# Indirect transfers pinned with their register moves, and the first four heads' queries loaded as float32 pairs, in a threshold-attention kernel

## The chip, the cores and the metric

The kernel runs on one core of one Trainium2 chip. The metric is the time of one execution on the device, in microseconds (us); less is better. Three timed runs of the kernel before gave 235.24, 236.1 and 237.11 us, median 236.1.

## The reference

```python
scores = np.einsum('bhqd,bhkd->bhqk', Q, K) * scale          # 8 batches, 12 heads, 512 x 512, dim 64
weights = np.exp(scores - np.max(scores, axis=-1, keepdims=True))
weights = weights / (np.sum(weights, axis=-1, keepdims=True) + 1e-10)
weights = np.where(weights > threshold, weights, 0)          # threshold 0.1
weights = weights / (np.sum(weights, axis=-1, keepdims=True) + 1e-10)
return np.einsum('bhqk,bhkd->bhqd', weights, V)
```

A softmax weight over 0.1 is rare among 512 keys, so nearly all rows of the output are zero.

## The kernel before

The kernel writes zeros over the whole output, finds the few rows that may hold a weight over the threshold, and works out those alone.

The 96 heads are handled in 48 pairs (`hp`) and 24 quads of heads (`hq`). For a pair, K arrives as float32 by two DMAs on the queue of SP (`load_k`, L209), is transposed on PE by matmuls with an identity (`do_ktr`, L333), copied from PSUM to SBUF as float32 (`kt`, by ACT at L317 or DVE at L319) and cast from there to float16 (`kf`, on POOL at L321). For a quad, Q arrives as float16 by one casting DMA on POOL's queue (`load_q`, L221), is brought into the layout of pairs (`qm`, POOL or DVE), transposed on PE (L370) and copied out (`qt`). Then, four times per pair, PE makes a 128 x 1024 tile of scores in PSUM (`sc`, L386), and ACT (L394, true exponential) or DVE (L396, an exponential by bits) makes the tile `e`; there are 192 such tiles. PE sums them against a small matrix (`groups`, L405), and DVE reduces the sums to one number per row (`stat`, L413).

For every eight heads (`j`, 12 of these groups) a chain of short steps follows, late behind the main stream: flags of the rows that pass, their rank, a list of row numbers (`idx`), then three indirect transfers, all on POOL's queue. The gather (L471) fetches the chosen rows of Q, their scores and exponentials are made anew (`xqk` L500, `xe` L507), the key is found (`junk` L518, `vidx` L525), the fetch (L536) brings the row of V into `vsel`, and the scatter (L542) writes it over the zeros of the output. A scatter waits for its `vsel` and for the two zero writes of its rows.

All steps are entered in a planner written in the kernel (`Schedule`): each has a list of engines with a cost in us, its predecessors, a due time, and the buffers that it takes and gives. The planner places the steps by greedy list scheduling; a list of random draws (`DRAWS`) shifts due times a little, and `LAG` sets how much later than the main stream the chains of the groups are due. The kernel then issues all steps in the order of the planned starts, and `keep` asks the recording layer to leave each engine's instructions in that order. An engine takes its instructions strictly in order, so one that waits holds up all behind it.

An indirect transfer comes with moves that set registers of POOL; only the transfer itself is given to `keep`. In the built program of before, the scatters do not stand where the planner put them: the plan has scatter `j` behind fetch `j+1` and two `kf` casts, while in the built order each scatter stands one to four instructions behind its own fetch. Gather and fetch have changed places in some groups.

At the start, K0 and K1 (the pairs of the first quad) are each loaded half by SP's and half by ACT's queue, and the first quad's Q by two casting DMAs on POOL. PE transposes K0 and K1 into one PSUM tile; DVE makes the two halves of `kt`, ACT casts both to `kf`; POOL and DVE make `qm`, PE transposes it, DVE makes `qt`. Then the first score tiles follow. Seven matmuls on zeros (`warm`, L263) run on PE before all of it.

Of the kernel before, what the change touches and what calls it, by code (L numbers as in the profile page):

```python
# [115 lines left out]
def kernel(  # L116
# [19 lines left out]
    nc = tc.nc  # L136
    B, H, S, D = Q.shape
    P = 128
    assert D == 64 and H % 4 == 0 and S == 4 * P and (B * H) % 8 == 0
    R = S // P  # L140
# [8 lines left out]
    f32 = mybir.dt.float32  # L149
    bf16 = mybir.dt.bfloat16  # L150
    f16 = mybir.dt.float16
# [35 lines left out]
    LAG, WARM = 8.0, 7  # L187
    DRAWS = (55125, 12429, 78892, 43664, 17346, 65358, 95610, 46971, 68712, 54930, 91140, 80100)
# [16 lines left out]
    T = {}  # L205

    def load_pair(dst, src, hp, other=nc.sync):
        for h, eng in ((0, nc.sync), (1, other)):
            eng.dma_start(out=dst[:, :, h, :], in_=src[hp][:, h])  # L209
# [6 lines left out]
    def load_q(hq, parts=1):  # L216
        q_sb = qload.tile([P, 4, R, D], f16)
        T["q", hq] = q_sb
        for i in range(parts):
            part = slice(i * 4 // parts, (i + 1) * 4 // parts)  # L220
            keep(nc.gpsimd.dma_start(out=q_sb[:, part].rearrange("p h r d -> p h (r d)"), in_=Q4[hq][:, part]))  # L221

    load_k(0, nc.scalar)
    load_q(0, 2)
    load_k(1, nc.scalar)
# [110 lines left out]
    def do_kev(hq, part, eng):  # L336
        if part != 1:
            kt = ktpool.tile([P, 2, S], f32)
            T["kt", hq] = kt
        n = slice(0, 2) if part is None else slice(part, part + 1)  # L340
        copy(eng, T["kt", hq][:, n], T["ktr", hq][:, n])
# [22 lines left out]
    def do_qtr(hq, part, eng):  # L364
        if part != 1:
            qp = mpsum.tile([P, 2, S], f16, name="smh", tag="sm")
            T["qtr", hq] = qp
        for n in range(2) if part is None else (part,):
            for r in range(R):
                keep(nc.tensor.matmul(T["qtr", hq][:, n, r * P:(r + 1) * P],  # L370
                                      lhsT=T["qm", hq][:, n, r].rearrange("p h d -> p (h d)"),
                                      rhs=identity_h[:], is_transpose=True, start=True, stop=True))

    def do_qev(hq, part, eng):
        if part != 1:
            qt = qtpool.tile([P, 2, S], f16)
            T["qt", hq] = qt
        n = slice(0, 2) if part is None else slice(part, part + 1)
        copy(eng, T["qt", hq][:, n], T["qtr", hq][:, n])
# [90 lines left out]
    def do_gather(j, eng):  # L470
        keep(nc.gpsimd.indirect_dma_start(  # L471
            out=qsel_bufs[j % NS][:], out_offset=None, in_=Qr,
            in_offset=bass.IndirectOffsetOnAxis(ap=T["idx", j][:, 0:1], axis=0),
            element_offset=j * 8 * S * D, bounds_check=8 * S - 1, oob_is_err=False))
# [60 lines left out]
    def do_fetch(j, eng):  # L535
        keep(nc.gpsimd.indirect_dma_start(  # L536
            out=T["vsel", j][:], out_offset=None, in_=Vr,
            in_offset=bass.IndirectOffsetOnAxis(ap=T.pop(("vidx", j))[:, 0:1], axis=0),
            element_offset=j * 8 * S * D, bounds_check=8 * S - 1, oob_is_err=False))

    def do_scatter(j, eng):
        i = nc.gpsimd.indirect_dma_start(  # L542
            out=Or, out_offset=bass.IndirectOffsetOnAxis(ap=T.pop(("idx", j))[:, 0:1], axis=0),
            in_=T.pop(("vsel", j))[:], in_offset=None, element_offset=j * 8 * S * D,
            bounds_check=8 * S - 1, oob_is_err=False)
        keep(i)
        T["scat", j] = i
# [24 lines left out]
    add("numbers", {"POOL": (1.5, 1.6)}, [("q", 0)], -3.0, do_numbers)  # L572
    add("casts", {"DVE": (1.3, 1.5)}, ["numbers"], 1.0, do_casts)
    for hq in range(NQ):
# [4 lines left out]
        for n, hp in enumerate(pairs):  # L579
            if hp < 2:  # L580
                add(("k", hp), {"SP": (0.7, 3.3)}, [], -30 + n, nothing)
            else:
                buf = [("ktr", hp - 6)] if hp >= 6 else [("ktr", max(0, hp // 2 - 1))]
                add(("k", hp), {"SP": (1.3, 4.0)}, buf, u0 - 26 + n, lambda e, hp=hp: load_k(hp))
        if hq == 0:
            add(("q", 0), {"POOL": (2.0, 4.5)}, [], -30, nothing)
        else:
            buf = [("qmix", 2 * hq - 5)] if hq >= 3 else [("qmix", 0)]
            add(("q", hq), {"POOL": (0.85, 5.5)}, buf, u0 - 20, lambda e, hq=hq: load_q(hq))
        add(("z", hq), {"SP": (2.0, 5.0)}, [("exp", 2 * hq, 0)], u0 + 4, lambda e, hq=hq: do_zero(hq, e))  # L590
        for n, hp in enumerate(pairs):
            add(("ktr", hp), {"PE": (0.44, 0.70)}, [("k", hp)] + (ahead if n == 0 else [("ktr", hp - 1)]), u0 - 9 + n * 0.1,
                lambda e, hp=hp: do_ktr(hp, e), takes=[("sc", ("ktr", hq))] if n == 0 else [])
            add(("qmix", hp), {"POOL": (0.57, 0.75), "DVE": (0.25, 0.40)}, [("q", hq)] + (ahead if n == 0 else [("qmix", hp - 1)]), u0 - 10,
                lambda e, hp=hp: do_qmix(hp, e), takes=[("qm", hq)] if n == 0 else [])
        if hq == 0:
            for n in range(2):
                add(("kev", 0, n), HALF, [("ktr", n)] + ([("kev", 0, 0)] if n else []), -8 + n, lambda e, n=n: do_kev(0, n, e),
                    takes=[] if n else [("kt", 0)], gives=[("sc", ("ktr", 0))])
                add(("qtr", 0, n), {"PE": (0.23, 0.44)}, [("qmix", n)] + ([("qtr", 0, 0)] if n else []), -8 + n,  # L600
                    lambda e, n=n: do_qtr(0, n, e), takes=[] if n else [("sm", ("qtr", 0))], gives=[("qm", 0)])
                add(("qev", 0, n), {"DVE": (0.35, 0.5), "ACT": (0.50, 0.72)}, [("qtr", 0, n)] + ([("qev", 0, 0)] if n else []), -7 + n,
                    lambda e, n=n: do_qev(0, n, e), takes=[] if n else [("qt", 0)], gives=[("sm", ("qtr", 0))])
        else:
            add(("kev", hq), UNIT, [("ktr", hp) for hp in pairs], u0 - 8, lambda e, hq=hq: do_kev(hq, None, e),
                takes=[("kt", hq)], gives=[("sc", ("ktr", hq))])
            add(("qtr", hq), {"PE": (0.45, 0.66)}, [("qmix", hp) for hp in pairs], u0 - 8, lambda e, hq=hq: do_qtr(hq, None, e),
                takes=[("sm", ("qtr", hq))], gives=[("qm", hq)])
            add(("qev", hq), {"DVE": (0.62, 0.80), "ACT": (0.93, 1.13)}, [("qtr", hq)], u0 - 7, lambda e, hq=hq: do_qev(hq, None, e),
                takes=[("qt", hq)], gives=[("sm", ("qtr", hq))])  # L610
        for n, hp in enumerate(pairs):
            kev, qev = (("kev", 0, n), ("qev", 0, n)) if hq == 0 else (("kev", hq), ("qev", hq))
            kf_engs = {"POOL": (0.60, 0.78)}
            if hq == 0:
                kf_engs = {"POOL": (0.60, 0.78), "DVE": (0.5, 0.7), "ACT": (0.5, 0.7)}
            add(("kf", hp), kf_engs, [kev] + ([("kf", hp - 1)] if n else []), u0 - 6 + 4 * n, lambda e, hp=hp: do_kf(hp, e),
                takes=[("kf", hq)] if n == 0 else [])
            for c in range(R):
                u = u0 + 4 * n + c
                add(("qk", hp, c), {"PE": (0.23, 0.45)}, [("kf", hp), qev], u - 3,  # L620
                    lambda e, hp=hp, c=c: do_qk(hp, c, e), takes=[("sc", ("qk", hp, c))],
                    gives=[("kf", hq), ("qt", hq)])
                add(("exp", hp, c), UNIT, [("qk", hp, c)], u,
                    lambda e, hp=hp, c=c: do_exp(hp, c, e), takes=[("e", (hp, c))], gives=[("sc", ("qk", hp, c))])
            for jj in range(C2):
                deps = [("exp", hp, c) for c in range(R)] if jj == 0 else [("d", hp, jj - 1)]
                add(("d", hp, jj), {"PE": (0.116, 0.31 if jj == C2 - 1 else 0.116)}, deps, u0 + 4 * n + 3 + 0.01 * jj,
                    lambda e, hp=hp, jj=jj: do_d(hp, jj, e), takes=[("sm", ("d", hp))] if jj == 0 else [],
                    gives=[("e", (hp, c)) for c in range(R)] if jj == C2 - 1 else [])
            add(("dred", hp), {"DVE": (0.61, 0.78)}, [("d", hp, C2 - 1)], u0 + 4 * n + 3.5,  # L630
                lambda e, hp=hp: do_dred(hp, e), gives=[("sm", ("d", hp))])
        qevs = [("qev", 0, 0), ("qev", 0, 1)] if hq == 0 else [("qev", hq)]
        add(("qsq", hq), SQUARE, qevs, u0 + 4, lambda e, hq=hq: do_square("q", hq, e), takes=[("qsq", hq)], gives=[("qt", hq)])
        add(("ksq", hq), SQUARE, [("kf", hp) for hp in pairs], u0 + 4, lambda e, hq=hq: do_square("k", hq, e),
# [144 lines left out]
```

## Time and profile before

| what | value |
|---|---|
| median of three runs | 236.1 us |
| the profiled execution's own time | 233.86 us |
| its span, first instruction to last | 232.0 us |
| mean granted clock of PE | 0.915 |
| busy: PE, DVE, ACT, POOL | 195.5, 186.8, 157.3, 125.7 us |
| weight loads of PE (PEld) | 126.3 us |
| first tile `e` starts, last one ends | 10.61, 209.06 us |
| indirect transfers, mean of one on POOL: gather, fetch, scatter | 1112, 1112, 1032 ns |

The profile is of one execution. Its span is 1.86 us less than that execution's own time, which in turn is 2.24 us under the median of the timed runs. Busy times are of the engines; the DMA engines run beside them. A line of the timeline gives the start in us, the duration, engine, line of the code, operation, tile written and tile read, and in brackets how long the engine had been idle just before and what ended that. In the chain of waits, each piece is the work, or the transfer, that the next one had to wait for; "issue" is time for which the profile shows no releaser. A q behind an engine's name is its queue, where instructions are issued and wait.

### The profile page before, as it was taken

The numbers are of one execution on the slowest core, as the hardware profiler recorded it, in microseconds if no ns is written. First come the engines' busy times: TensorE is split into PE (matmuls) and PEld (weight loads), VectorE is DVE, ScalarE is ACT, GpSimd is POOL, SyncE is SP. The second block draws the span as 40 slices with busy tenths as digits, with TensorE's granted clock in tenths as the row PEclk, the third lists the DMA queues.
The fourth block names the chain that finished last, engine by engine and source line by source line (L and its number), as shares of the span: only waits on it lengthen the run. The fifth ranks groups of instructions, "written<-read, shape, count | busy, mean of one in ns | idle before, by whom it ended". The sixth has DMA issues, their size and how long they took to land.

```text
span 232.0 us, 7237 instructions
## 1 busy us (share of the span) xinstructions
PE 195.5 (84%) x2997; PEld 126.3 (54%) x2997; DVE 186.8 (81%) x327; ACT 157.3 (68%) x186; POOL 125.7 (54%) x204
## 2 busy tenths in 40 slices
PE   6498998999669988998999799899889999798130
PEld 2255665666347655674666466566566657455000
DVE  5568999989566898899689798799889997998420
ACT  2378779787646786779659579698868787880010
POOL 4617335664473738573764663875584736413541
PEclk9779999999956999999799999999999999998555
DMA  6999999999989996547257186455563000000000
GB/s 129 202 233 360 198 202 359 322 263 335 328 258 285 288 214 109 86 105 129 33 113 141 43 120 124 99 78 110 81 125 79 11 0 7 9 5 4 9 2 13
DMA packets 68019, 32.54 MB, mean 140 GB/s; under 512 B 52278, under 2 KB 64706, under 8 KB 67984
## 3 DMA queue, kind: packets, MB, share of 16 engines
q1 hardware_dynamic: 53088, 24.91, 39.7%
q0 software_dynamic: 13840, 6.88, 22.8%
q8 instruction: 24, 0.39, 0.7%
q10 hardware_dynamic: 1056, 0.26, 0.5%
q14 instruction: 11, 0.09, 0.1%
HBM read 25.95 MB, written 12.98 MB: 168 GB/s over the span
## 4 chain that ended last, share of the span: by engine, by line
PE 48%; DVE 17%; DMA 11%; issue 8%; ACT 8%; POOL 6%; POOLq 0%; ACTq 0%; DVEq 0%
PE sm L405 15%; PE sc L386 14%; PE sc L333 8%; DMA vsel<-in_V_dram,vidx 8%; DVE e L396 7%; ACT e L394 5%; PE smh L370 3%; PE sm L429 3%; PE sm L500 3%; DVE stat L413 2%; DMA k_sb<-in_K_dram 2%; POOL out_dram L542 2%; DVE kt L319 2%; DVE ksq L353 2%; DMA qsel<-in_Q_dram,idx 1%
## 5 line engine op out<-in xcount | busy, mean ns | idle before, releaser
L394 ACT ACTIVATE e<-sc 128x1024 bf16<-128x1024 f32 x125 | 122.7, 1026 | 30.2 <-PE sc L386 27.3
L396 DVE TENSOR_SCALAR e<-sc 128x1024 int16<-128x1024 f32 x67 | 81.2, 1218 | 2.9 <-PE sc L386 1.7
L386 PE MATMUL sc<-qt,kf 64*128 64x512 f16 x384 | 67.4, 399 | 8.2 <-DVE e L396 3.6
L405 PEld LDWEIGHTS <-e 128*128 128x128 bf16 x1536 | 53.9, 100 | 25.5 <-issue 20.7
L405 PE MATMUL sm<-groups,e 128*128 128x64 bf16 x1536 | 63.3, 196 | 4.5 <-ACT e L394 1.8
L321 POOL CAST kf<-kt 128x512 f16<-128x512 f32 x46 | 29.2, 648 | 40.1 <-ACT kt L317 23.5
L413 DVE TENSOR_REDUCE stat<-sm 128x8 f32<-128x512 f32 x48 | 32.9, 686 | 13.8 <-PE sc L386 6.5
L333 PE MATMUL sc<-identity_f,k_sb 128*128 128x128 f32 x192 | 31.8, 296 | 1.4 <-DMA k_sb<-in_K_dram 1.4
L386 PEld LDWEIGHTS <-kf 64*128 64x128 f16 x384 | 17.0, 94 | 26.8 <-issue 18.2
L333 PEld LDWEIGHTS sc<-identity_f,k_sb 128*128 128x128 f32 x192 | 22.0, 149 | 7.2 <-issue 3.8
L221 POOL DMA_DIRECT2D q_sb<-in_Q_dram x25 | 20.7, 827 | 5.8 <-POOL qm L321 2.7
L321 POOL COPY qm<-q_sb 128x512 f16<-128x512 f16 x36 | 22.8, 653 | 1.8 <-DMA q_sb<-in_Q_dram 1.6
L542 POOL DMA_INDIRECT out_dram<-vsel,idx x12 | 12.4, 1032 | 20.7 <-DMA vsel<-in_V_dram,vidx 18.7
L370 PE MATMUL smh<-identity_h,qm 128*128 128x128 f16 x192 | 15.5, 221 | 4.6 <-DVE qt L319 2.0
L471 POOL DMA_INDIRECT qsel<-in_Q_dram,idx x12 | 13.3, 1112 | 9.4 <-DVE qb L479 3.6
L317 ACT COPY kt<-sc 128x1024 f32<-128x1024 f32 x13 | 13.2, 1014 | 6.0 <-PE sc L333 4.8
L536 POOL DMA_INDIRECT vsel<-in_V_dram,vidx x12 | 13.3, 1112 | 6.8 <-POOL vidx L525 2.6
L507 ACT ACTIVATE xe<-sm 128x512 f32<-128x512 f32 x12 | 7.2, 603 | 14.3 <-PE sm L500 14.3
L317 ACT COPY qt<-smh 128x1024 f16<-128x1024 f16 x12 | 12.2, 1013 | 6.8 <-PE smh L370 4.5
L319 DVE COPY kt<-sc 128x1024 f32<-128x1024 f32 (+1 forms) x12 | 13.5, 1132 | 3.9 <-PE sc L333 3.9
L353 DVE TENSOR_SCALAR ksq<-kf 128x1024 int16<-128x1024 int16 x24 | 13.8, 576 | 3.4 <-POOL kf L321 3.4
L370 PEld LDWEIGHTS <-qm 128*128 128x128 f16 x192 | 11.4, 98 | 8.4 <-DVE qm L319 3.4
(85 smaller groups left out, 176.8 us busy)
## 6 DMA issues: line engine op xcount, KB each, us to landing
out_dram<-zero SPq DMA_DIRECT2D x24, 512.0 KB, 7.0
k_sb<-in_K_dram SPq DMA_DIRECT2D x94, 128.0 KB, 4.8
q_sb<-in_Q_dram POOLq DMA_DIRECT2D x23, 256.0 KB
k_sb<-in_K_dram ACTq DMA_DIRECT2D x2, 128.0 KB
q_sb<-in_Q_dram POOLq DMA_DIRECT2D x2, 128.0 KB
qsel<-in_Q_dram,idx POOLq DMA_INDIRECT x12
vsel<-in_V_dram,vidx POOLq DMA_INDIRECT x12
out_dram<-vsel,idx POOLq DMA_INDIRECT x12
```

Of the source, the lines that this page charges most:

```text
L221: keep(nc.gpsimd.dma_start(out=q_sb[:, part].rearrange("p h r d -> p h (r d)"), in_=Q4[hq][:, part]))
L317: keep(nc.scalar.copy(dst, src))
L319: keep(nc.vector.tensor_copy(dst, src))
L321: keep(nc.gpsimd.tensor_copy(dst, src))
L333: keep(nc.tensor.matmul(T["ktr", hq][:, n, r * P:(r + 1) * P], lhsT=k_sb[:, r, :, :].rearrange("p h d -> p (h d)"), rhs=identity_f32[:], i ...
L353: keep(nc.vector.tensor_scalar(sq[:].bitcast(i16), src[:].bitcast(i16), 0x7FFF, 2, op0=ALU.bitwise_and, op1=ALU.logical_shift_right))
L370: keep(nc.tensor.matmul(T["qtr", hq][:, n, r * P:(r + 1) * P], lhsT=T["qm", hq][:, n, r].rearrange("p h d -> p (h d)"), rhs=identity_h[:], ...
L386: keep(nc.tensor.matmul(sc[:, h, :], lhsT=T["kf", hq][ps, n, c * P:(c + 1) * P], rhs=T["qt", hq][ps, n, :], start=True, stop=True))
L394: keep(nc.scalar.activation(e[:], sc[:], ACTF.Exp, scale=scale))
L396: keep(nc.vector.tensor_scalar(e[:].bitcast(i16), sc[:], BITS_A, BITS_B, op0=ALU.mult, op1=ALU.add))
L405: keep(nc.tensor.matmul(T["d", hp][:, j, :], lhsT=T["e", hp, c][:, h, qt * P:(qt + 1) * P], rhs=groups[:], start=(c == 0), stop=(c == R - 1)))
L413: keep(nc.vector.tensor_reduce(T["stat", j][:, n, :], T.pop(("d", hp))[:], axis=AX.X, op=ALU.max))
```

## The change

1. **Pin.** A helper `indirect` issues gather, fetch and scatter. It puts an ordering edge to the last POOL instruction already issued on everything that the transfer issues, its register moves too. In the built order of the changed kernel the three kinds of transfer stand on POOL where the planner put them: scatter `j` behind fetch `j+1`, or next to it. At the end of the program stand fetch 11, scatter 9, scatter 11, scatter 10.
2. **First quad.** Q of the first four heads comes as float32 in two pairs (`load_first_q`), like K, through the same six `k_sb` buffers: SP's queue holds K0 (first half), Q0 (first half), K1, Q1, then K2, K3; ACT's queue the second halves of K0 and Q0. POOL loads Q from the second quad on. PE transposes K0 and Q0 into the two halves of one `sc` tile, K1 and Q1 into another (`do_first_tr`); `kf`, `qt` and `kt` are each copied directly out of this tile (`do_first_ev`). In the built order PE takes K0, K2, Q0, K3, K1, then the first score tile, the second quad's `qm`, Q1, then the other score tiles. ACT takes the first half of `kt`, the `kt` of K2 and K3, the second half of `kt`, then its first `e`.
3. **Planner.** `LAG` goes from 8 to 10, and twelve draws are replaced by fourteen others, so that the whole order of steps is another one. ACT now has 131 of the tiles `e` and DVE 61 (before 125 and 67); DVE has 8 of the `qm` copies (before 12). The casts of the row numbers (`casts`) are due later.

The diff, cut to its core:

```diff
-    LAG, WARM = 8.0, 7
-    DRAWS = (55125, 12429, 78892, 43664, 17346, 65358, 95610, 46971, 68712, 54930, 91140, 80100)
+    LAG, WARM = 10.0, 7
+    DRAWS = (50494, 69804, 89651, 71919, 28206, 70018, 95892, 48669, 78702, 5004, 56538, 37674, 78297, 48453)
...
+    def indirect(**args):
+        before = next(i for i in reversed(nc.cur_bb.bb.instructions) if i.engine == mybir.EngineType.Pool)
+        with tc.issue_after(before):
+            return keep(nc.gpsimd.indirect_dma_start(**args))
...
+    def load_first_q(hp, other=nc.sync):
+        q_sb = kload.tile([P, R, 2, D], f32, name="k_sb")
+        load_pair(q_sb, Qp, hp, other)
+        T["q32", hp] = q_sb

     load_k(0, nc.scalar)
-    load_q(0, 2)
-    load_k(1, nc.scalar)
+    load_first_q(0, nc.scalar)
+    load_k(1)
+    load_first_q(1)
...
+    def do_first_tr(n, which, eng):
+        if which == 0:
+            sc = spsum.tile([P, 2, S], f32, name="sc", tag="sc")
+            T["first", n] = sc
+        src = T.pop((("k", "q32")[which], n))
+        for r in range(R):
+            keep(nc.tensor.matmul(T["first", n][:, which, r * P:(r + 1) * P], lhsT=src[:, r, :, :].rearrange("p h d -> p (h d)"),
+                                  rhs=identity_f32[:], is_transpose=True, start=True, stop=True))
+
+    def do_first_ev(n, what, eng):
+        pool, dtype = {"kt": (ktpool, f32), "kf": (kfpool, f16), "qt": (qtpool, f16)}[what]
+        if n == 0:
+            dst = pool.tile([P, 2, S], dtype, name=what)
+            T[what, 0] = dst
+        copy(eng, T[what, 0][:, n], T["first", n][:, int(what == "qt")])
...
     def do_gather(j, eng):
-        keep(nc.gpsimd.indirect_dma_start(
+        indirect(
...
     def do_scatter(j, eng):
-        i = nc.gpsimd.indirect_dma_start(
+        T["scat", j] = indirect(
...
-        keep(i)
-        T["scat", j] = i
...
-    add("casts", {"DVE": (1.3, 1.5)}, ["numbers"], 1.0, do_casts)
+    add("casts", {"DVE": (1.3, 1.5)}, ["numbers"], 12.0, do_casts)
+    for n in range(2):
+        for which, at in enumerate(((3.5, 4.5), (6.0, 7.3))[n]):
+            add((("k", "q32")[which], n), {"SP": (0.01, at)}, [], -30 + n, nothing)
...
-                buf = [("ktr", hp - 6)] if hp >= 6 else [("ktr", max(0, hp // 2 - 1))]
+                if hp >= 8:
+                    buf = [("ktr", hp - 6)]
+                else:
+                    buf = [("first", (hp - 4) // 2, hp % 2)] if hp >= 4 else []
                 add(("k", hp), {"SP": (1.3, 4.0)}, buf, u0 - 26 + n, lambda e, hp=hp: load_k(hp))
```

## The prediction

> **What bounds the kernel now.** I read the page first, then the chain of waits, POOL's timeline where that chain runs through a transfer, a table of busy times by stretch, and the start and the end of the timeline.
>
> The page's account of the chain:
>
> ```profile
> PE 48%; DVE 17%; DMA 11%; issue 8%; ACT 8%; POOL 6%; POOLq 0%; ACTq 0%; DVEq 0%
> ```
>
> No engine is the bound all along: PE leads, but 11% of the span is spent on transfers, and the page's next line gives 8% to one of them, the fetch of `vsel`. In order of time, the chain's longest such place is this:
>
> ```profile
> 57.56 6.19 DMA vsel<-in_V_dram,vidx
> 63.75 0.28 issue
> 64.03 1.04 POOL out_dram L542
> 65.10 0.35 POOL flags L417
> 65.44 0.57 POOL kf L321
> 66.04 0.81 DVE ksq L353
> 66.84 1.15 DVE e L396
> ```
>
> POOL's timeline shows why a fetch of 128 rows stops the others: the scatter behind it holds the cast `kf`, for which the next score tiles wait.
>
> ```profile
> 57.56 1.16 POOL L536 DMA_INDIRECT vsel<-in_V_dram,vidx  x1 [0.40 <-POOL vidx L525]
> 59.02 1.02 POOL L471 DMA_INDIRECT qsel<-in_Q_dram,idx  x1 [0.30 <-DVE qsq L353]
> 60.05 0.62 POOL L321 CAST kf<-kt 128x512 f16<-128x512 f32 x1
> 64.03 1.04 POOL L542 DMA_INDIRECT out_dram<-vsel,idx  x1 [3.36 <-DMA vsel<-in_V_dram,vidx]
> 65.10 0.35 POOL L417 TENSOR_SCALAR flags<-stat 128x32 bf16<-128x32 f32 x1
> 65.38 0.63 POOL L321 CAST kf<-kt 128x512 f16<-128x512 f32 x1
> ```
>
> What that costs is read from busy times by stretch (columns: PE, PEld, DVE, ACT, POOL, granted clock, DMA share, GB/s):
>
> ```profile
> 24.00:56.00 32.00, 30.89 (x521) 20.68 (x518) 29.73 (x44) 26.15 (x29) 15.49 (x25) 1.00 1.11 284
> 56.00:72.00 16.00, 12.15 (x180) 8.88 (x179) 10.01 (x17) 8.88 (x9) 7.75 (x12) 0.71 1.00 274
> 56.00:208.00 152.00, 138.50 (x2206) 91.31 (x2205) 130.78 (x206) 115.13 (x137) 88.01 (x139) 0.96 0.56 117
> ```
>
> DVE and ACT share the exponentials, so their sum measures the pace. From 24 to 56 us, before the first scatter, it is 55.88 us in 32, or 1.746 per us. From 56 to 72 it is 18.89, worth 10.8 us at that pace: 5.2 us are lost, and the granted clock falls to 0.71. From 56 to 208 it is 245.91, worth 140.8 of 152 us: 11.2 us lost in all.
>
> **Step A, the scatters move.** POOL sat idle before scatters for 18.7 us waiting for `vsel` (waits of POOL). Of that 6.6 are behind 208 us (2.19, 2.11, 2.29), 12.1 before. In the changed order one whole group's work stands between a fetch and its scatter, about 16 us (12 groups in the 198 us from the first `e` to the last), while the landings on the chain took 6.19, 5.73 and 3.02 us; so these waits go. The scatter, its register moves (29 ns each) and its semaphore waits are moved past `kf`, `qm`, the next gather and fetch and the Q loads on POOL, and past K loads and zero writes on SP's queue, on which it also waits; being later only eases that. Its own 1.03 us stays on POOL, in another place. Behind it the cast `kf` is next to be late: it already waits 39.8 us for `kt`, which is not POOL's doing. The gain lies between 5.2 us (the one stretch with the 3.36 us wait) and 11.2 us (all that is lost after 56). The other waits before 208 (3.71, 0.90, 2.26, 0.95, 0.89) lie in the same 152 us, and 12.1 us of waits is nearer the upper end: I take 10.0 gained.
>
> **Step B, the start.** Two casting loads (0.91 and 0.77 us on POOL), the `qm` copies and eight float16 transposes (221 ns) go; eight float32 ones (296 ns) come, and `kf` is cast straight from PSUM. But PE is now to transpose K2 between K0 and Q0, and K3 before K1, and these loads stand behind all of the first quad on SP's queue:
>
> ```profile
> L209 SPq DMA_DIRECT2D k_sb<-in_K_dram x8: 605/644/1074, 0.8 to 6.3; - x8
> DMA to landing us min/median/max: 5.1/5.2/5.3
> ```
>
> This is tile `k_sb` in the first 7 us: SP's eighth load starts at 6.3 and one takes 5.2 us to land. K2 takes the seventh and eighth place, so it lands at 11.5; the tenth ends its issue at 8.68 (SP's timeline: ten from 0.81, 7.87 long), starts about 8.0, and K3 lands at 13.2. The queue's eight semaphores had to be free before the seventh load in the old order too. Four transposes took 1.12 us at 12.31, with the granted clock at 0.50, and PE will have idled from 5.1 on. So K2 is done at 12.6, Q0 13.7, K3 14.8, K1 15.9; then DVE's cast of K1 and ACT's of the same tile, about 0.6 each (`kt` 128x512: 1.29 for two), stand before ACT's first `e`: 17.2 us, where it was 10.61. That is 6.6 late. Part returns:
>
> ```profile
> 17.00 1.02 ACT L394 ACTIVATE e<-sc 128x1024 bf16<-128x1024 f32 x1 [0.55 <-PE sc L386]
> 17.06 1.21 DVE L396 TENSOR_SCALAR e<-sc 128x1024 int16<-128x1024 f32 x1
> 20.63 1.94 ACT L394 ACTIVATE e<-sc 128x1024 bf16<-128x1024 f32 x2 [0.48 <-PE sc L386]
> ```
>
> In the old order the eighth tile starts at 17.06 and the ninth at 20.63, because `kt`, `kf` and `qt` of the second quad came in between. In the new order K2 and K3 are transposed, copied and cast before or beside the first tiles: 3.4 us back. Net cost 3.2. Bounds: at full clock four transposes took 0.66 (at 6.54), which makes it 4 x 0.46 = 1.8 less, so 1.4; with the slowest landing (8.6, below) 6.6. I take 3.2, since both rows used are those of the same place in the queue.
>
> The Trainium skill, "TensorE: Matmul & The Clock Gate", in "HAM oscillation — how this bites in real kernels", warns of idle gaps of PE over about 3.4 us; the clock of 0.50 after the gaps at the start agrees. It speaks against this change's start; by it the sum stays as it is, by the full-clock row it would be 1.8 less.
>
> **Step C, the end.** The last transfers before:
>
> ```profile
> 224.48 1.10 POOL L536 DMA_INDIRECT vsel<-in_V_dram,vidx  x1 [0.47 <-POOL vidx L525]
> 227.88 1.02 POOL L542 DMA_INDIRECT out_dram<-vsel,idx  x1 [2.29 <-DMA vsel<-in_V_dram,vidx]
> ```
>
> Now scatter 9 stands between them, covered by the 2.29 us wait (uncovered it would cost 1.03), and scatter 10 follows scatter 11: 1.03 us more. Scatter 9 no longer stands ahead of gather 11, but that gather came only 0.27 us after its `idx` (215.48, 215.75). I take 1.0 lost, between 0.7 and 2.1.
>
> **Step D, LAG and draws.** Six tiles go from DVE (1218 ns) to ACT (1026 ns), four `qm` copies from DVE (336 ns) to POOL, the less busy engines: 1.15 + 1.34 us off the sum, 1.4 us at 1.746 per us. What else the new order does has no row; the stretch from 112 to 136 is 3.3 us below the pace with only a 0.90 us scatter wait in it, so orders can differ by that much either way. I take 1.0 gained, between 4 gained and 3 lost.
>
> **Sum.** -10.0 + 3.2 + 1.0 - 1.0 = -6.8. The profiled execution took 233.86 us with a span of 232.0; I expect a span of 225.2 and 227.1 for it. It lies 2.2 under the median of the runs, 236.1, so the median becomes 229.3.
>
> **Rivals.**
>
> *The waits move (0.20).* POOL stays in the way: it also waits 7.1 us for `junk`, 6.6 for `xe`, 3.4 for `idx`, each with casts queued behind. Then only the big stall's 5.2 us comes back: 236.1 - 5.2 + 3.2 = 234.1. Against it: in 24 to 56 us POOL waited mostly for `kt`, at full pace.
>
> *Loads of the start share the DMA engines (0.15).* POOL's loads of three more quads are issued from about 2.3 us on, beside SP's. In the first 20 us, landing took
>
> ```profile
> DMA to landing us min/median/max: 5.1/6.5/8.6
> ```
>
> At 8.6 K3 lands at 16.6 instead of 13.2, all else follows, and the time is 229.3 + 3.4 = 232.7. For it: the wider spread where POOL's loads and zero writes run. Against it: in the old order too, POOL loaded beside K1. The Trainium skill, "DMA: Bandwidth & Descriptors", "Queues, rings and completion order", says that each DMA engine takes turns between queues packet by packet, which is this rival; the spread agrees.
>
> *The stalls covered nothing but idle time (0.08), the slower side.* PE is busy 84% of the span and 48% of the chain; if PE's work is the bound, A gives nothing: 236.1 + 3.2 + 1.0 - 1.0 = 239.3. It decides where A is under 0.8. Against it: PE itself had 12.15 us of work in the 16 us of the stall.
>
> *All comes back (0.17).* A gives 11.2 and the new order 4: 236.1 - 11.2 + 3.2 + 1.0 - 4.0 = 225.1.
>
> That the pin does nothing is excluded by the built order.
>
> **How the numbers follow.** My forecast, 229.3, has 0.40, with 227 to 231.5 as its own range. The range of 224 to 235 leaves out the slower side (0.08), the upper end of the moved waits and the lower end of the best case (0.05 each). Under 1% nothing can be told from no change here. Faster by over 1% (under 233.7): 0.40 + 0.17, 0.14 of the shared loads and 0.07 of the moved waits: 0.78. Within 1%: the rest of these two, 0.14. Slower (over 238.5): 0.08.
>
> **What would show it.** A: POOL's idle time before scatters under 3 us up to 208, `kf` casts no longer behind them, the clock at 1.0 from 56 to 72, and a pace of about 1.75 there. B: first `e` near 17, PE waiting for K2 at about 11, ninth tile less than 1.5 us behind the eighth. C: three scatters in a row at the end, the last 1 us behind scatter 11. The prediction is wrong if the pace after 56 us stays at 1.62, or if the first `e` comes after 21.

## The result, and the profile after

The changed kernel took 239.76 us (median of 20 runs, 236.58 to 241.76), the kernel before 235.36 beside it: 1.0151 of its time, 95% interval [1.0119, 1.0184]. Ratios here and below compare the executions of each kernel that lie within 1.5% of its fastest, so they differ a little from the quotients of the medians. The change is slower by over 1%, 10.5 us above the forecast of 229.3 and outside the range. The profiled execution took 238.4 us, its span is 236.4 (before 232.0). Its chain by engine, from the page:

```profile
PE 62%; DVE 12%; ACT 7%; issue 7%; DMA 6%; SPq 2%; POOL 2%; POOLq 1%; ACTq 0%; DVEq 0%
```

Transfers fell from 11% to 6% of the chain, POOL from 6% to 2%. Busy times by stretch (columns as before):

```profile
56.00:72.00 16.00, 14.50 (x220) 9.17 (x217) 13.98 (x22) 12.63 (x15) 9.99 (x17) 1.00 1.10 295
56.00:208.00 152.00, 141.07 (x2251) 91.88 (x2250) 135.38 (x207) 118.80 (x144) 91.75 (x147) 0.99 0.58 125
```

The pace, the busy time of DVE and ACT together per us, is 26.61 / 16 = 1.663 from 56 to 72 (1.181 before) at a clock of 1.00. Over 56 to 208 it is 254.18 / 152 = 1.672, still below the 1.746 reached before 56. POOL's waits have no row in which a scatter waits for `vsel`; what is left before scatters is this:

```profile
POOL out_dram L211 <- issue: 5.9, 12, 1.5
```

The start, from the timeline:

```profile
5.16 7.22 SPq L215 DMA_DIRECT2D k_sb<-in_K_dram  x4
14.70 1.09 PE L343 MATMUL sc<-identity_f,k_sb 128*128 128x128 f32 x4 [9.68 <-DMA k_sb<-in_K_dram]
19.52 6.79 ACT L415 ACTIVATE e<-sc 128x1024 bf16<-128x1024 f32 x7
```

SP took 7.22 us to issue the four loads of K2 and K3 (each half a pair). PE, which takes K2 next after K0, stood still for 9.68 us, and the first `e` is at 19.52 (before 10.61).

The end, POOL and PE:

```profile
212.96 1.03 POOL L211 DMA_INDIRECT out_dram<-vsel,idx  x1 [0.78 <-issue]
214.01 0.58 POOL L500 TENSOR_TENSOR qb<-qsel,half 128x128 f32<-128x128 f32 x1
214.65 0.47 PE L507 MATMUL sm<-identity_f,qb 128*128 128x128 f32 x1 [2.09 <-POOL qb L500]
215.48 1.93 PE L521 MATMUL sm<-kt,xq 128*32 128x512 f32 x8 [0.35 <-ACT xq L327]
217.34 0.66 PE L477 MATMUL sm<-row_no,oh 128*128 128x5 f16 x8
218.99 1.25 POOL L211 DMA_INDIRECT qsel<-in_Q_dram,idx  x1 [0.51 <-DVE idx L487]
227.45 1.09 POOL L211 DMA_INDIRECT vsel<-in_V_dram,vidx  x1 [0.41 <-POOL vidx L546]
228.85 1.04 POOL L211 DMA_INDIRECT out_dram<-vsel,idx  x1 [0.30 <-issue]
231.39 0.99 POOL L211 DMA_INDIRECT out_dram<-vsel,idx  x1 [1.50 <-issue]
232.69 0.97 POOL L211 DMA_INDIRECT out_dram<-vsel,idx  x1 [0.30 <-issue]
```

The last `e` ends at 210.11. Split 10 (`qb`, which parts the gathered rows of group 10) is now on POOL behind scatter 8, where before it was on DVE; PE waits for it, does the products of group 10 and only then `idx` 11 (L477), so gather 11 starts 8.88 us behind the last `e`. The three last rows are scatters 9, 11 and 10.

Four numbers carry the rest, read off the tiles `e` in each profile: when the first, ninth and sixteenth start, and how long it is from the sixteenth's start to the last one's end ("middle") and from there to the end of the work ("tail").

| profile | first | ninth | 16th | middle | tail |
|---|---|---|---|---|---|
| before | 10.61 | 20.63 | 24.71 | 184.4 | 22.8 |
| changed, on record | 19.52 | 25.28 | 30.79 | 179.3 | 26.2 |
| pin alone, e1 | 10.34 | 20.55 | 24.62 | 170.7 | 23.6 |
| changed, e10 | 18.57 | 24.33 | 29.84 | 173.0 | 26.6 |
| before, e11 | 12.24 | 22.68 | 26.76 | 183.4 | 22.5 |
| pin alone, e12 | 10.63 | 21.77 | 25.71 | 173.2 | 23.8 |
| pin alone, e15 | 12.17 | 23.38 | 27.32 | 173.2 | 23.6 |
| changed, e16 | 18.62 | 24.52 | 30.02 | 171.8 | 26.6 |

The rows with an e are experiments of the next section; e10, e11 and e12 ran on one chip, e15 and e16 on another. Each row is one execution. Kernels with the old start reach the sixteenth tile anywhere from 24.6 to 27.3 us, so a difference of 1 or 2 us between two single rows says little.

### The profile page after: what moved, and what is told of

Same layout as the page of the kernel before. It is cut to its first block, busy times and chain, and to the rows that moved or that the text cites. A ratio compares the mean times of both kernels' runs of the same rounds, so it can differ in the third digit from the quotient of the medians.

```text
span 236.4 us, 7242 instructions
## 1 busy us (share of the span) xinstructions
PE 194.2 (82%) x2997; PEld 125.5 (53%) x2997; DVE 185.0 (78%) x317; ACT 158.3 (67%) x190; POOL 126.3 (53%) x206
## 3 DMA queue, kind: packets, MB, share of 16 engines
q0 software_dynamic: 13296, 6.62, 21.2%
## 4 chain that ended last, share of the span: by engine, by line
PE 62%; DVE 12%; ACT 7%; issue 7%; DMA 6%; SPq 2%; POOL 2%; POOLq 1%; ACTq 0%; DVEq 0%
PE sc L407 18%; PE sm L426 16%; PE sc L343 9%; ACT e L415 6%; PE sm L521 5%; PE smh L392 5%; DVE e L417 4%; DMA k_sb<-in_K_dram 4%; PE sm L450 3%; PE sm L477 3%; SPq L215 2%; PE sm L507 1%; DVE qsq L377 1%; DVE junk L539 1%; DVE stat L434 1%
## 5 line engine op out<-in xcount | busy, mean ns | idle before, releaser
L415 ACT ACTIVATE e<-sc 128x1024 bf16<-128x1024 f32 x131 | 127.5, 1027 | 27.8 <-PE sc L407 23.7
L417 DVE TENSOR_SCALAR e<-sc 128x1024 int16<-128x1024 f32 x61 | 73.8, 1216 | 4.2 <-PE sc L407 3.6
L426 PEld LDWEIGHTS <-e 128*128 128x128 bf16 x1536 | 51.7, 98 | 23.3 <-issue 20.1
L426 PE MATMUL sm<-groups,e 128*128 128x64 bf16 x1536 | 60.9, 193 | 3.4 <-ACT e L415 1.2
L225 POOL DMA_DIRECT2D q_sb<-in_Q_dram x23 | 18.8, 819 | 16.8 <-DVE qm L329 12.2
L327 ACT COPY kt<-sc 128x1024 f32<-128x1024 f32 (+1 forms) x14 | 13.3, 952 | 18.1 <-PE sc L343 12.6
L534 POOL TENSOR_SCALAR tv<-sum 128x1 f32<-128x1 f32 x12 | 2.9, 239 | 29.0 <-ACT xe L528 29.0
L329 DVE COPY kt<-sc 128x1024 f32<-128x1024 f32 x11 | 13.4, 1219 | 2.3 <-PE sc L343 2.1
L521 PE MATMUL sm<-kt,xq 128*32 128x512 f32 x96 | 14.5, 680 | 0.8 <-DVE xq L329 0.4
L377 DVE TENSOR_SCALAR qsq<-qt 128x1024 int16<-128x1024 int16 x24 | 14.4, 605 | 0.1
```

What stands on the lines that cost most here:

```text
L225: keep(nc.gpsimd.dma_start(out=q_sb[:].rearrange("p h r d -> p h (r d)"), in_=Q4[hq]))
L377: keep(nc.vector.tensor_scalar(sq[:].bitcast(i16), src[:].bitcast(i16), 0x7FFF, 2, op0=ALU.bitwise_and, op1=ALU.logical_shift_right))
L415: keep(nc.scalar.activation(e[:], sc[:], ACTF.Exp, scale=scale))
L417: keep(nc.vector.tensor_scalar(e[:].bitcast(i16), sc[:], BITS_A, BITS_B, op0=ALU.mult, op1=ALU.add))
L426: keep(nc.tensor.matmul(T["d", hp][:, j, :], lhsT=T["e", hp, c][:, h, qt * P:(qt + 1) * P], rhs=groups[:], start=(c == 0), stop=(c == R - 1)))
L521: keep(nc.tensor.matmul(sc[sl, :], lhsT=xq[:, sl], rhs=T["kt", 2 * j + n // 2][:, n % 2, :], start=True, stop=True, tile_position=(0, n * ...
```

## The experiments

The first theory was that the pin is worth some 10 us as forecast and that the new order loses it at start and end ("order"); its rival that the pin is worth only about 4 ("cover"). Ratios are to the kernel before on the same chip; e1 to e4 ran on one chip, e5 to e8 on another.

**e1: the pin alone.** The kernel before with the helper and nothing else.

```diff
+    def indirect(**args):
+        before = next(i for i in reversed(nc.cur_bb.bb.instructions) if i.engine == mybir.EngineType.Pool)
+        with tc.issue_after(before):
+            return keep(nc.gpsimd.indirect_dma_start(**args))
...
-        keep(nc.gpsimd.indirect_dma_start(
+        indirect(
```

> The kernel before with the pin alone: the three indirect transfers take their planned places on POOL, nothing else changes. If the scatters' waits were really worth the 10 us of step A and the new LAG and draws lost most of that again (theory: order), the time is about 10 us below the kernel before, near 226. If step A was priced too high because the other engines had work left during most of the waits (theory: cover), it gains only what the changed kernel gained between its 16th tile and its last, about 4 us: near 231.5. If the pin itself costs, it is at or above the kernel before.

Measured: 222.38 us, ratio 0.9617 [0.9538, 0.9696]. Stretches of its profile (the last `e` ends at 195.31):

```profile
56.00:72.00 16.00, 14.52 (x240) 10.34 (x239) 15.76 (x26) 12.96 (x15) 9.60 (x17) 1.00 1.13 329
56.00:195.00 139.00, 134.41 (x2232) 89.39 (x2230) 131.40 (x206) 115.81 (x139) 86.71 (x138) 1.00 0.60 126
```

The pace is 1.795 in the first and 1.778 in the second, where the kernel before had 1.181 and 1.618. The middle falls by 13.7 us against the first profile of before, and by 10.2 between e11 and e12 on one chip. The stalls had covered work, not idle time.

**e2: the change without the pin.** The transfers are issued as before.

```diff
-        before = next(i for i in reversed(nc.cur_bb.bb.instructions) if i.engine == mybir.EngineType.Pool)
-        with tc.issue_after(before):
-            return keep(nc.gpsimd.indirect_dma_start(**args))
+        i = nc.gpsimd.indirect_dma_start(**args)
+        keep(i)
+        return i
```

> The changed kernel without the pin: gather, fetch and scatter are given to keep as before, and the scatters stand right behind their own fetches again. Theory order: about 10 us slower than the changed kernel, near 250. Theory cover: about 4 slower, less the 1.3 us that scatter 10 behind scatter 11 costs at the end: near 242.5. If the pin costs: faster than the changed kernel.

Measured: 248.02 us, 1.0689 [1.0611, 1.0767]. POOL in the place of the first scatter:

```profile
64.84 1.08 POOL L209 DMA_INDIRECT vsel<-in_V_dram,vidx  x1 [0.43 <-DVE vidx L546]
73.88 1.04 POOL L209 DMA_INDIRECT out_dram<-vsel,idx  x1 [7.96 <-DMA vsel<-in_V_dram,vidx]
```

One scatter stops POOL for 7.96 us. "Order" holds, "cover" is out: without the pin, the rest of the change costs 6.9%. That 248 meets the 250 named is in part luck: 250 was 10 us above the 239.8 on record, but e5, e10 and e16 put the changed kernel near 1.00 of the kernel before on other chips, so the pin is worth some 7% in this order of steps against 4% in the old one. Its middle is 195.2 us.

**e3: PE's order at the start.** The changed kernel with PE's K2 and K3 behind the first pair's score tiles. `later` takes steps out of the planned order and puts them behind the step named last.

```diff
...
+    later([("ktr", 2), ("ktr", 3)], ("qk", 0, 3))
+    later([("kev", 1), ("kf", 2), ("kf", 3)], ("exp", 0, 2))
```

> The changed kernel with PE's transposes of K2 and K3 (and the copies made of them) moved behind the first pair's score tiles; the loads stay as they are. If PE's order at the start is what costs, the first tile e starts near 11.5 us (K1 lands at 9.5) instead of 19.5, and the time falls by 3 to 5 us, to about 236: not by all of 8, since the second quad now comes later. If the loads themselves are the bound, the ninth tile waits for K3 as before and the time stays within 1 us of the changed kernel.

Measured: 228.11 us, 0.984 [0.977, 0.991].

```profile
10.98 1.03 ACT L415 ACTIVATE e<-sc 128x1024 bf16<-128x1024 f32 x1
```

The first `e` is back at its old place, 8.5 us earlier than on record, but the sixteenth only 2.8 earlier (28.02): the second quad still comes late. Against e2, which has the start of the changed kernel on this chip (18.66 and 29.94), it is 7.7 and 1.9.

**e4: POOL's loads held.** POOL copies two numbers out of K1 before it issues the Q loads of quads 1 to 3, so these wait for K1.

```diff
+        if hq == 1:
+            held = consts.tile([P, 1], f32, name="held")
+            keep(nc.gpsimd.tensor_copy(held[:], T["k", 1][:, 0, 0, 0:1]))
+            keep(nc.gpsimd.tensor_copy(held[:], T["k", 1][:, 0, 1, 0:1]))
```

> The changed kernel with POOL's three early loads of Q held back until K1 has landed (two one-column copies on POOL that read K1 stand ahead of them). If these loads took the bandwidth from SP's queue, K2 and K3 land at about 11 to 13 us as the prediction had it, instead of 14.6 and 15.5, the first tile e starts near 16.5, and the time falls by 2 to 3 us, to about 237. If SP's queue is slow for another reason, K2 still lands at 14 or later and the time is the same or, with the second quad's Q later, above.

Measured: 230.0 us, 0.9955 [0.9912, 0.9997]. The same places as above:

```profile
4.86 2.65 SPq L215 DMA_DIRECT2D k_sb<-in_K_dram  x4
9.47 1.08 PE L347 MATMUL sc<-identity_f,k_sb 128*128 128x128 f32 x4 [4.18 <-DMA k_sb<-in_K_dram]
15.28 0.49 DVE L333 COPY qm<-q_sb 128x512 f16<-128x512 f16 x2 [3.07 <-DMA q_sb<-in_Q_dram]
16.89 1.03 ACT L419 ACTIVATE e<-sc 128x1024 bf16<-128x1024 f32 x1
```

SP's four issues take 2.65 us instead of 7.22, and PE has K2 at 9.47 instead of 14.70. The fair comparison is e2, with the start of the changed kernel on this chip: there the four issues take 5.45 us and PE has K2 at 13.77. So POOL's three loads had cost K2 4.3 us. The two loads of K2 themselves, in e2 and then in e4, from the view of tile `k_sb` about their issue:

```profile
DMA to landing us min/median/max: 8.1/8.2/8.3
DMA to landing us min/median/max: 3.8/3.8/3.9
```

But the held load of Q now arrives late, and DVE waits for it with K1's cast queued behind: the wait moved to another engine's queue, and the sixteenth tile stays at 30.74.

**e5: the changed kernel again.** Nothing is edited; the middle of e3 and e4 (172.8 and 171.4) had been much shorter than on record.

> The changed kernel once more, unaltered, beside the others. Its profile put the stretch from the sixteenth tile to the last at 179.3 us, while the same order with the loads held took 171.4 in another profile. If the middle really is as fast as with the loads held (theory 'start and tail lose it'), this profile shows 171 to 173 there and the time is 1.00 of the kernel before or a little under. If the late loads of the start spoil the middle too (theory 'the start goes on hurting'), it shows 177 to 180 again and the ratio is 1.01 to 1.02.

Measured: 231.03 us, 1.0007 [0.9968, 1.0047], middle 171.4. The slow middle is not the program's alone.

**e6: the tail's order.** The changed kernel, with these lines (`on` gives a step to another engine):

```diff
...
+    on(("split", 10), "DVE")
+    later([("split", 10)], ("dred", 47))
+    later([("idx", 11), ("half", 11), ("idxev", 11), ("gather", 11), ("check0", 11)], ("oh", 11))
+    later([("xtr", 10), ("xev", 10), ("xqk", 10), ("xexp", 10), ("tv", 10)], ("gather", 11))
+    later([("scatter", 9)], ("fetch", 10))
+    later([("scatter", 10)], ("fetch", 11))
```

> The changed kernel with another order of the last twelve microseconds only: split 10 on DVE, idx 11 with half, idxev and gather ahead of the ninth-to-last block's transposes and products (xtr, xqk 10), the check's first half behind idxev 11, scatter 9 ahead of fetch 11 and scatter 10 ahead of scatter 11. Theory 'the tail's order costs it': gather 11 is issued some 3.4 us behind the last flags instead of 7.05, the fetch 8.5 us behind that, one scatter less at the end (1.3): 26.2 us from the last tile to the end become 21 to 22, and the time falls by 4.5 to 5 us against the unaltered one. Rival 'the tail is set by transfers': 24 to 26 and at most 1.5 us.

Measured: 225.43 us, 0.9762 [0.9697, 0.9828], on the chip of e5. POOL's end (the last `e` ends at 202.14):

```profile
207.21 1.05 POOL L211 DMA_INDIRECT qsel<-in_Q_dram,idx  x1 [1.03 <-DVE idx L487]
216.30 1.10 POOL L211 DMA_INDIRECT vsel<-in_V_dram,vidx  x1 [0.42 <-POOL vidx L546]
217.70 1.03 POOL L211 DMA_INDIRECT out_dram<-vsel,idx  x1 [0.31 <-issue]
219.69 1.00 POOL L211 DMA_INDIRECT out_dram<-vsel,idx  x1 [0.96 <-DMA vsel<-in_V_dram,vidx]
```

Gather 11 comes 5.07 us behind the last `e` instead of 8.88, scatter 10 lies in the wait for the last fetch, and the tail is 21.2 us. The order had cost it, not the transfers; which of the moves gave how much was not tried apart.

**e7: LAG alone.** The pinned kernel of e1 with `LAG` at 10.

> The kernel before with the scatters pinned (0.962 of the kernel before by itself) and LAG at 10 instead of 8, its own draws kept: what the later due time alone does to the order. My step for LAG and draws said -1.0 us with -4 to +3. If a later due time helps, 0.955 and 16th to last tile under 170.7; if any new order costs something because the old one was searched for, 0.97 to 0.985.

Measured: 229.23 us, 0.9896 [0.981, 0.9981], against 0.9602 to 0.9617 for the pin alone. A later due time by itself costs some 3% here. Its profile, of an execution 2.1 us over the median, is longer than e1's in the middle (176.6) and in the tail (26.8). Whether the old draws no longer fit it, or the due time is at fault, was not tried apart.

**e8: start and tail together.** The changed kernel with e6's lines, POOL's loads of quads 2 and 3 held until K1, and the whole first quad ahead of the second on all engines:

```diff
...
+    on(("exp", 0, 1), "DVE")
+    later([("first", 0, 0), ("first", "kf", 0), ("first", "kt", 0), ("first", 0, 1), ("first", "qt", 0), ("k", 4), ("k", 5), "numbers",
+           ("qk", 0, 0), ("exp", 0, 0), ("qk", 0, 1), ("exp", 0, 1), ("qk", 0, 2), ("exp", 0, 2), ("first", 1, 0),
+           ("first", "kf", 1), ("qk", 0, 3), ("exp", 0, 3), ("first", 1, 1), ("first", "qt", 1), ("first", "kt", 1),
+           ("qmix", 2), ("qmix", 3), ("qtr", 1), ("qev", 1), ("qk", 1, 2), ("exp", 1, 2), ("qk", 1, 1), ("exp", 1, 1),
+           ("ktr", 2), ("ktr", 3), ("kev", 1), ("kf", 2), ("kf", 3)], ("q", 3))
...
```

> The changed kernel with an order of the start that follows the landings (first pair's four score tiles ahead of the second pair's transposes, quad 1's transposes behind the first two tiles of pair 1), POOL's loads of quads 2 and 3 held until K1 has landed, and the tail of the run beside it. Theory 'order on the in-order engines loses it': first e near 8.5, ninth tile 17 to 19, sixteenth 23 to 25, 170 to 173 to the last tile, 21 to 22 behind it: a span of 216 to 219, 0.93 to 0.94 of the kernel before. Rival 'the start is set by the bytes of the loads': the ninth tile stays at 21 or later and the span at 221 or more.

Measured: 227.24 us, 0.9758 [0.9668, 0.9848]: no better than e6, and far from the 0.93 to 0.94 named. The first `e` is at 8.64, but the ninth at 22.2, because the second quad's `kf` comes only at 18.73. My order gained at the first tile and lost it at the ninth; that bytes set the ninth is not shown.

**e9: pin and tail.** The pinned kernel of e1 with e6's six lines.

> The kernel before with the scatters pinned and the tail's order mended as it was for the changed kernel (split 10 on DVE, idx 11 to gather 11 ahead of xtr 10, scatter 9 ahead of fetch 11, scatter 10 ahead of scatter 11). If the start is the larger loss of the change and the tail the other, this is the fastest of all: 23.6 us from the last tile to the end become 21 to 22, so 1.5 to 2.5 us under the pin alone, 0.95 to 0.955 of the kernel before. If the tail gains nothing here, 0.96.

Measured: 220.82 us, 0.9516 [0.9472, 0.9561], tail 22.4: the fastest of all kernels here, ahead of both.

**e10, e11, e12, on the chip of e9:** the changed kernel, the kernel before and the pin alone, unaltered.

> The changed kernel unaltered, on one chip with the three others. It took 239.8 us in the comparison of record and 231.0 in the second one, with 179.3 and 171.4 us between the sixteenth and the last tile. Theory 'start and tail lose it, the chip adds the rest': 171 to 172 again here and 230 to 232 us. Rival 'the program has two speeds': 176 to 180 and 236 to 240.

> The kernel before unaltered, for its profile beside the pinned one of the same chip. Theory 'the pin gives the middle back': 181 to 185 us between the sixteenth and the last tile against 170 to 172 with the pin, start and tail the same to 0.5 and 1 us. Rival 'the earlier 184.4 was that chip's': 174 to 178.

> The kernel before with the scatters pinned and nothing else, once more: 0.955 to 0.97 of the kernel before, 170 to 172 us between the sixteenth and the last tile. Against the changed kernel on the same chip it should be 7 to 10 us faster, of which the sixteenth tile (24.6 against 30.3 to 30.8) makes 5.7 and the stretch behind the last tile (23.6 against 26.2 to 26.6) makes 3; if the middle of the changed kernel is slower of its own, the difference is over 12.

Measured: the changed kernel 231.24 us, 0.9959 [0.9926, 0.9992], middle 173.0, tail 26.6; the kernel before 234.54 us, 1.0078 [1.0036, 1.0121], middle 183.4, tail 22.5; the pin 224.26 us, 0.9602 [0.9501, 0.9702], middle 173.2. Three things came out otherwise than expected: the pin's middle lies above 170 to 172, the sixteenth tiles of e11 and e12 differ by 1.1 us, not by 0.5 at most, and the sixteenth tile of the changed kernel is 4.1 us behind the pin's (29.84, 25.71) and 3.1 behind that of the kernel before (26.76), not 5.7. The kernel before differs from itself by 0.8% between two sets of runs, which is how far single ratios can be trusted.

**e13: the changed kernel a fourth time, and e14: e3 and e6 together,** on another chip.

> The changed kernel unaltered once more. In the comparison of record it took 239.8 us with 179.3 us between the sixteenth and the last tile; in two later comparisons 231.0 and 231.2 us with 171.4 and 173.0. If the slower middle belongs to where it ran, 230 to 232 us and 171 to 174 here, or 236 to 240 with 177 to 180 and pauses of 0.8 us and more in which ACT and DVE both stand still. Anything between would speak for a middle whose speed varies from run to run.

> The changed kernel with both repairs that gained alone: PE's transposes of K2 and K3 behind the first pair's score tiles (and kev 1, kf 2, kf 3 behind the third e), and the mended tail. If start and tail are separate losses, the gains add: first e near 11, sixteenth tile near 28, 171 to 173 to the last, 21 to 22 behind it: a span of 221 to 223, 0.955 to 0.97 of the kernel before, level with the pin alone. If they overlap, 0.975 to 0.985.

Measured: e13 239.58 us, 1.0226 [1.0186, 1.0266], middle 182.5; e14 233.67 us, 0.993 [0.9887, 0.9973], tail 21.8. The slow middle is back, and e14 has it too (182.3). Between the two, the repairs gain 5.9 us; alone, e6 gained 5.6 against e5 and e3 some 3 across chips, so the gains add up only in part.

**e15: the pin a third time, and e16: the changed kernel a fifth time,** on one chip.

> The kernel before with the scatters pinned and nothing else, beside the changed kernel on one chip. Two comparisons gave 0.9617 and 0.9602 of the kernel before and 170.7 and 173.2 us between the sixteenth and the last tile. If the places where ACT and DVE both stand still belong to the changed kernel's order, it is 0.955 to 0.965 here too, whatever the changed kernel takes; if any order suffers them on such a chip, 0.98 or more where the changed kernel is at 1.015 or more.

> The changed kernel unaltered, beside the pin alone. Either 230 to 232 us with no place after 25 us in which ACT and DVE both stand still for 0.9 us, or 238 to 241 us with a standstill of 2.0 us about 21 to 23 us behind the ninety-sixth-last tile's stretch (near 100 to 104 us) as in the comparison of record.

Measured: 222.57 us, 0.9598 [0.9545, 0.965], and 231.38 us, 0.9977 [0.9939, 1.0016]. This chip shows the short middle, so it does not tell how the pin alone fares where the changed kernel is slow.

**Where the slow middle loses it.** One place of the program in three profiles of the same kernel. On record:

```profile
102.16 0.69 DVE L434 TENSOR_REDUCE stat<-sm 128x8 f32<-128x512 f32 x1 [2.53 <-PE sc L407]
102.20 1.94 ACT L415 ACTIVATE e<-sc 128x1024 bf16<-128x1024 f32 x2 [2.07 <-PE sc L407]
```

e13:

```profile
104.03 0.69 DVE L434 TENSOR_REDUCE stat<-sm 128x8 f32<-128x512 f32 x1 [2.52 <-PE sc L407]
104.07 1.94 ACT L415 ACTIVATE e<-sc 128x1024 bf16<-128x1024 f32 x2 [2.06 <-PE sc L407]
```

e16, where DVE goes on from its `e` at once and ACT runs four tiles without a gap, and its stretch:

```profile
95.61 1.21 DVE L417 TENSOR_SCALAR e<-sc 128x1024 int16<-128x1024 f32 x1
96.79 0.69 DVE L434 TENSOR_REDUCE stat<-sm 128x8 f32<-128x512 f32 x1
95.38 3.88 ACT L415 ACTIVATE e<-sc 128x1024 bf16<-128x1024 f32 x4 [1.11 <-PE sc L407]
```

```profile
56.00:200.00 144.00, 138.07 (x2251) 90.03 (x2248) 135.52 (x207) 118.79 (x145) 91.71 (x146) 1.00 0.60 127
```

On record and in e13 ACT and DVE stand still together for 2.0 us there. Both have a second standstill of 0.8 us some 30 us later at the same step, and a third, of 0.9 and 1.1 us, some 20 us earlier and one tile apart; e16 has none of the three. Its pace from 56 to 200 is 254.31 / 144 = 1.766; the prediction had put about 1.75 on 56 to 72 us, where e16 has 28.34 / 16 = 1.771. What PE lacks there the profile calls "issue".

## Why the prediction was wrong, by its steps

**On record, profile against profile,** the start cost 6.1 us (forecast 3.2), the middle gave 5.1 (forecast 10.0 of step A and 1.0 of step D), and the tail cost 3.4 (forecast 1.0). The two profiles come from different comparisons, and the experiments divide the miss better.

**Step A (-10.0) was right in mechanism and nearly in size.** The pin alone gives 0.9598 to 0.9617 in three comparisons, 9.0 to 9.5 us of 236.1, inside 5.2 to 11.2. POOL no longer waits for `vsel`, but for 0.97 us at the end of e1; the clock is 1.0 from 56 to 72, and the pace there is 1.66 to 1.80. The rivals "waits move" and "stalls covered nothing but idle time" fall with e1 and e2. The latter named 239.3, and 239.76 was measured; that is luck, as its reason was that step A gives nothing.

**Steps B (+3.2) and D (-1.0), together +2.2, cost 5.6 to 5.9 us.** On the two chips that ran both, the changed kernel is 0.0357 and 0.0379 above the pin alone, 8.4 and 8.9 us of 236.1, and the tail (step C) takes 2.8 and 3.0 of that; the intervals of the ratios leave some 1 to 2.5 us either way. How the rest divides between start and order is not settled. By the sixteenth tile the start costs 3.1 us in e10 against e11, 5.3 in e2 against e1, and 6.1 on record, all inside the bounds of 1.4 to 6.6. The middle of the changed kernel (171.4 to 173.0 where it is short) and of the pin (170.7 to 173.2) overlap, so step D's gain of 1.0 does not show, and its sign is open; e7 has `LAG` by itself as a loss.

**What failed in step B is K2's landing at 11.5.** PE's order and the half clock came as forecast (four transposes 1.09 us, forecast 1.12), and from K2's start to the first `e` it took 4.8 us, forecast 5.7. But PE could start K2 only at 14.70 on record, and at 13.67 to 14.78 in the five profiles of the changed kernel. The issue came early enough (K2's second half at 5.54 in e2, forecast 6.3); the landing took 8.1 to 8.3 us there, not 5.2. The step took 5.2 from the only two early loads of SP whose landing the profile of before has, issued at 2.18 and 4.20, when POOL had issued two casting loads of 128 KB; in the changed kernel it issues three of 256 KB. It left these to a rival, "loads of the start share the DMA engines", which had the mechanism, as e4 shows, and by the Trainium skill ("DMA: Bandwidth & Descriptors", "Queues, rings and completion order") queues take turns packet by packet on each engine; the trace agrees (landings of 3.8 us without POOL's loads against 8.2 with them). The eight semaphores, which the step also names, did not hold the issues on record: the landings that the four loads of K2 and K3 wait for were in by 5.43 us. The second part, tiles 1 to 16 without a gap, came true for the ninth (4.7 late after 8.9 at the first), but 1.4 us were lost again by the sixteenth.

The step also says that the half clock at the start agrees with the warning that it cites. But the two gaps of PE ahead of it in the profile of before were 1.42 and 2.02 us, shorter than the gap warned of, and the clock was down to 0.62 from 8 to 9 us, within the second; so these rows do not bear it out. The 0.50 used in the sum is measured.

**Step C (+1.0) was mis-sized: 3.0 us** (tail 26.6 in e16 against 23.6 in e15 and e1; 3.4 on record against before). Scatter 10 last was foreseen and costs its 1.30. Not foreseen was the order of group 10 against group 11: split 10 on POOL behind a scatter, and `idx` 11 on PE behind group 10's products. The step looked at POOL's last rows alone. e6 gets 5.3 us of tail back.

**Sum, where the middle is short:** the pin's 9.4 and 9.5 us less 8.4 and 8.9 leave 1.0 and 0.5 gained, and the ratios of e5, e10 and e16 are 1.0007, 0.9959 and 0.9977. Of the forecast gain of 6.8 us, 3.4 to 3.7 went in start and order and 1.8 to 2.0 in the tail; the pin itself gave 0.5 to 0.6 less than forecast.

**On record 7.5 us more are lost in the middle** (179.3 against 171.8), at the same places of the program, in two of five comparisons (e5, e10, e13 and e16 each ran on a chip of its own). Without them the time would have been about 232 us, within 224 to 235, though still 3 us over the forecast. No step foresaw that. The prediction's own signs of failure, a pace that stays at 1.62 or a first `e` after 21, did not come either (1.672 and 19.52). The three standstills make 3.8 of the 7.5 us. In the same two comparisons the kernel before is slower too, but by 1% (medians 235.4, against 232.5 to 233.7), and SP's four issues at the start take 7.22 and 7.46 us, against 5.39 to 6.13 in e5, e10 and e16. Whether that has the same cause is not shown. It is open what holds PE there, and whether the pin alone loses the same on such a chip: no comparison put the pin beside a slow middle.

## What to carry to other kernels

An indirect write that waits for its own fetch stops everything queued behind it on an in-order engine; putting one group's work between the two was worth 4%. A change that moves steps must be read on every engine at both ends of the run, where nothing hides a wait: here a load taken too early by PE and a few steps in another order at the end cost most of what the pin gave, and mending both won 5.9 us back (e14 against e13). Price a new load with the other queues' loads running beside it, not from rows in which less ran there. And take two kernels' difference from one chip, over several executions: single profiles put the cost of this start anywhere from 3.1 to 6.1 us.

## What the runs showed of the hardware

One program took 231 us in three comparisons and 239.6 to 239.8 in two others, while the kernel before took 232.5 to 235.4 beside them. On record, about half of what the middle takes longer is standstills, at the same instructions in both, 2.0 us the longest. Behind that one the granted clock falls:

```profile
103.00:104.00 1.00, 0.72 (x4) 0.65 (x4) 1.00 (x3) 1.00 (x2) 0.32 (x1) 0.70 0.01 3
104.00:106.00 2.00, 2.00 (x10) 0.93 (x8) 1.25 (x5) 1.17 (x2) 0.58 (x1) 0.50 0.07 17
106.00:108.00 2.00, 2.00 (x42) 1.61 (x40) 1.87 (x2) 1.02 (x1) 1.00 (x3) 0.80 1.00 179
```

With 1.00 and 0.50 as the two values, these rows hold 0.6, 2.0 and 0.8 us at half clock, 3.4 us in all; e13 has as much behind the same standstill (0.50 from 106 to 108, 0.66 from 108 to 110). In e14 the standstill of 2.0 us at the same place leaves the clock at 1.00, so the pause alone does not decide it. The pause is well under the gap of about 3.4 us for which the Trainium skill ("TensorE: Matmul & The Clock Gate", "HAM oscillation — how this bites in real kernels") warns; PE was not wholly idle in it. The other surprise is SP's queue: an issue of a load, 0.66 us each in e4 (2.65 for four), took 1.8 us each on record (7.22 for four) while POOL's casting loads were under way.
